# Chunk inverses of a recurrent mixer from blocks of sixteen rows, with shared products in its chunk steps

## The chip, the core and the metric

The kernel runs on one core of a Trainium2 chip. A core has five engines that work side by side, each through its own queue of instructions: TensorE (PE in the profile; its weight loads stand apart as PEld), VectorE (DVE), ScalarE (ACT), GpSimd (POOL) and SyncE (SP), which here issues the transfers. The time is the device time of one execution in microseconds.

## The reference, cut to what matters

The model is a long chain of layers over 512 tokens of width 1024. The change touches one of them, a mixer with 16 heads of width 64 whose state runs through the tokens:

```python
def step(state, inp):                      # state: heads x 64 x 64
    r_t, w_t, k_t, v_t, a_t, b_t = inp
    sa = jnp.einsum('bhij,bhj->bhi', state, a_t)
    state = (state * w_t[:, :, None, :] + sa[..., None] * b_t[:, :, None, :]
             + v_t[..., None] * k_t[:, :, None, :])
    y_t = jnp.einsum('bhij,bhj->bhi', state, r_t)
    return state, y_t
...
_, ys = lax.scan(step, state0, seq_inputs)  # one step per token
```

Then `ys` is normalised by head, gets a bonus term, is gated and goes through an output projection.

## The kernel before

The scan is done in chunks of 64 tokens. Within a chunk the corrections `sa` of its 64 tokens depend on each other through a triangular 64 x 64 matrix, and the kernel multiplies by that matrix's inverse. Two heads stand side by side on the 128 partitions (a head pair), so there are eight pairs `c` and eight chunks. Work comes in four units `u`: half `h = u // 2` of the tokens (four chunks `n`), and pairs 0 to 3 or 4 to 7. A unit has four parts:

- `rwkv_prep` and `rwkv_chunks`, for each pair: decays, keys and receptances (in `kr`), then products on TensorE into `G`, which holds for each chunk four 64 x 64 blocks: by `BK` (update vectors or keys) against `kr` (keys or receptances). L1583 are these products.
- `rwkv_inverse1`: the unit's 32 triangular blocks (4 pairs x 2 heads x 4 chunks) go through DRAM (`md`) so that a partition holds half of a matrix, 32 x 32. VectorE (GpSimd for unit 2) inverts these by 31 steps of two operations each (L1619, L1621). The results go back through DRAM into `G`, and a copy into `A11`.
- `rwkv_inverse2`: the off-diagonal 32 x 32 blocks, by two rounds of 32 small products (L1646, L1651), with a copy between them (L1648) and one after (L1653).
- `rwkv_steps`: four chunks in order, and in each the unit's four pairs. All its products go through the helper `mm` and show as L1665. For a pair and chunk they are, by the tiles on which they show: the residual, from the old state (`SB,kr`) and from `V` by two products (`ws`, 64*64), copied to `R` by L1688; the inverse applied (`R,ws`), copied by L1692; the new state, from the old one by a product with the identity (`SB,cst`, 128*128) and two products (`ws`, 128*64), scaled and copied by L1703; the output, from the old state (`SB,kr`) and two products (`ws`, 128*64), copied by L1710.

The instructions are written in the order of `rwkv` (L1465 to L1484), and a planner then orders each engine's queue by priorities and a simulated time; `steps` raises the priority of `rwkv_steps`. So preps, `rwkv_post` (normalising and gating of a finished unit) and the first products of the output projection lie in each queue among the steps. The steps start when the value projection `vproj` is done, since `UV` and unit 2's working set reuse the space of its inputs. A tag with n buffers (`bufs`) is handed out in turn: steps take two of three `mm` banks of the accumulators, the inverse's products the only `av` bank.

## Time and profile before

| | |
|---|---|
| median of 3 runs | 3906.36 us (3902.74 to 3907.86) |
| the profiled execution | 3908.79 us, span 3907.0 us |
| mean granted TensorE clock, of full speed | 0.956 |
| busy: PE, PEld | 3738.4 us (96%), 3000.4 us (77%) |
| busy: DVE, ACT, POOL | 1753.8 us (45%), 1507.1 us (39%), 1642.4 us (42%) |

Times in the rows count from the start of the span. An engine is busy while an instruction of it runs; matmuls are pipelined, so that one row's length is more than its distance to the next. An fp32 product shows as two records, and "x4" in a row is four records in a run. `64*128` means 64 rows of weights and 128 columns. The granted clock is 1.00 at 2.4 GHz and 0.50 at 1.2 GHz. A shown tile can be a larger buffer: `ws`, `wse` and `hn` are the units' working sets with `G`, `BK` and `UV`, `cst` the constants, `SB` the states, `av`, `mm`, `sc` and `tr` the accumulator banks.

### The profile page before, as it was taken

To read this page: it belongs to the slowest core of one execution; us is meant where nothing else is said; L and a number is where in the kernel's file an instruction comes from. 1 tells how busy PE (TensorE), PEld (TensorE's weight loads), DVE (VectorE), ACT (ScalarE), POOL (GpSimd) and SP (SyncE) were. 2 spreads that over 40 slices of the span, in tenths; PEclk is the share of its full clock that TensorE was granted. 3 is DMA by queue.
4 is the path that set the end of the run, shared out by engine and by line. 5 is a ranking of instruction groups with operands and counts; after the bars stand their busy time and mean duration, and the time that the engine had idled before them with its cause. 6 is when DMAs were issued, how large, how long until landed. Compare 5 with 4: busy or idle time off the path is not lost.

```text
span 3907.0 us, 48377 instructions
## 1 busy us (share of the span) xinstructions
PE 3738.4 (96%) x18540; PEld 3000.4 (77%) x18540; DVE 1753.8 (45%) x3587; ACT 1507.1 (39%) x2677; POOL 1642.4 (42%) x900
## 2 busy tenths in 40 slices
PE   9999999999999999999998899999899899799998
PEld 8766777888896677778886777888676777688887
DVE  4553254533545424544436655222568545534123
ACT  4433333433344333334334634332454433343322
POOL 4422436444453233444444563444534321543444
PEclk9999999999999999999998999999999557899999
DMA  5311214233342122232221332222222311321222
GB/s 190 116 54 49 89 60 135 87 97 97 120 152 81 55 67 71 87 114 97 97 95 62 99 106 76 86 93 95 99 85 88 73 41 42 124 102 63 96 97 87
DMA packets 148952, 354.10 MB, mean 91 GB/s; under 512 B 50080, under 2 KB 60864, under 8 KB 148464
## 3 DMA queue, kind: packets, MB, share of 16 engines
q1 hardware_dynamic: 148448, 350.18, 27.6%
q8 instruction: 146, 2.39, 0.3%
q0 software_dynamic: 272, 0.82, 0.1%
q14 instruction: 86, 0.70, 0.1%
HBM read 332.56 MB, written 18.38 MB: 90 GB/s over the span
## 4 chain that ended last, share of the span: by engine, by line
PE 76%; DVE 9%; DMA 5%; POOL 4%; ACT 3%; issue 3%; SPq 0%; POOLq 0%; DVEq 0%; ACTq 0%
PE mm L322 13%; PE mm L323 13%; PE mm L324 13%; PE mm L384 5%; PE mm L383 5%; PE mm L385 5%; PE mm L1665 4%; POOL wlo L285 2%; PE av L383 2%; PE av L385 2%; PE av L384 2%; PE sc L823 2%; PE av L652 1%; PE tr L843 1%; ACT whi L284 1%
## 5 line engine op out<-in xcount | busy, mean ns | idle before, releaser
L285 POOL TENSOR_TENSOR wlo<-wst,whi 128x1024 fp32r<-128x1024 f32 (+2 forms) x524 | 1260.2, 2408 | 1784.2 <-PE mm L324 900.9
L284 ACT ACTIVATE whi<-wst 128x1024 fp32r<-128x1024 f32 (+2 forms) x524 | 548.7, 1048 | 1100.0 <-DMA wst<-in_wu 153.1
L322 PE MATMUL mm<-xTh,whi 128*128 128x512 f32 (+1 forms) x2208 | 833.1, 379 | 13.1 <-ACT whi L284 10.1
L323 PE MATMUL mm<-xTl,whi 128*128 128x512 f32 (+1 forms) x2208 | 835.8, 379 | 0.6
L324 PE MATMUL mm<-xTh,wlo 128*128 128x512 f32 (+1 forms) x2208 | 833.2, 378 | 0.0
L322 PEld LDWEIGHTS mm<-xTh,whi 128*128 128x128 f32 x2208 | 416.6, 190 | 99.8 <-ACT whi L284 11.5
L324 PEld LDWEIGHTS mm<-xTh,wlo 128*128 128x128 f32 x2208 | 418.4, 190 | 84.0 <-issue 8.5
L323 PEld LDWEIGHTS mm<-xTl,whi 128*128 128x128 f32 x2208 | 418.5, 190 | 81.8 <-issue 6.8
L867 DVE SCALAR_TENSOR_TENSOR fup<-mm,vec,fup 128x510 f32<-128x510 f32 (+1 forms) x176 | 131.0, 747 | 220.1 <-ACT fup L865 217.1
L829 ACT ACTIVATE P<-sc,sm 128x128 f32<-128x128 f32 x192 | 100.7, 525 | 203.6 <-DVE sm L827 203.4
L826 DVE TENSOR_TENSOR sc<-sc,cst 128x128 f32<-128x128 f32 x192 | 56.3, 297 | 271.1 <-PE sc L825 256.4
L1160 DVE TENSOR_TENSOR relu<-relu,mm 128x512 f32<-128x512 f32 x64 | 43.8, 687 | 297.6 <-ACT relu L1159 297.6
L384 PE MATMUL mm<-wlo,ph 128*128 128x512 f32 x396 | 156.6, 395 | 0.0
L385 PE MATMUL mm<-whi,pl 128*128 128x512 f32 x396 | 154.6, 395 | 0.0
L383 PE MATMUL mm<-whi,ph 128*128 128x512 f32 x396 | 154.4, 396 | 0.0
L384 PE MATMUL mm<-wlo,xTh 128*128 128x512 f32 (+1 forms) x360 | 137.4, 382 | 5.2 <-POOL wlo L285 5.2
L385 PE MATMUL mm<-whi,xTl 128*128 128x512 f32 (+1 forms) x360 | 136.4, 380 | 0.0
L383 PE MATMUL mm<-whi,xTh 128*128 128x512 f32 (+1 forms) x360 | 132.8, 382 | 3.6 <-ACT whi L284 3.6
L1180 DVE TENSOR_TENSOR work<-work,mm 128x512 f32<-128x512 f32 x60 | 41.2, 687 | 168.1 <-PE mm L385 160.2
L968 PE MATMUL tr<-dg,work 128*128 128x128 f32 x384 | 61.9, 328 | 46.9 <-DVE rsq L416 16.0
L297 POOL TENSOR_TENSOR wres<-wst,wres 128x512 fp32r<-128x512 f32 (+1 forms) x56 | 83.7, 1512 | 37.1 <-ACT wres L296 32.2
L968 PEld LDWEIGHTS tr<-dg,work 128*128 128x128 f32 x384 | 58.8, 240 | 50.3 <-issue 33.6
(580 smaller groups left out, 7431.4 us busy)
## 6 DMA issues: line engine op xcount, KB each, us to landing
wst<-in_wu SPq DMA_DIRECT2D x88, 512.0 KB, 3.6
wst<-in_wmu SPq DMA_DIRECT2D x64, 512.0 KB, 3.6
wst<-in_wmd SPq DMA_DIRECT2D x64, 512.0 KB, 3.6
wst<-in_wg SPq DMA_DIRECT2D x48, 512.0 KB, 3.6
wst<-in_wn SPq DMA_DIRECT2D x44, 512.0 KB, 3.6
wst<-in_wa SPq DMA_DIRECT2D x24, 512.0 KB, 3.6
wst<-in_wb SPq DMA_DIRECT2D x24, 512.0 KB, 3.6
wst<-in_wd SPq DMA_DIRECT2D x24, 512.0 KB, 3.6
```

The source lines that it names most:

```text
L284: nc.scalar.activation(hi, st, AF.Copy)
L285: nc.gpsimd.tensor_sub(lo, st, hi.bitcast(F32))
L322: mm(out, lh, rh, start=start, stop=False)
L323: mm(out, lh, rl, start=False, stop=False)
L324: return mm(out, ll, rh, start=False, stop=stop)
L383: mm(o, xh, hi[:, s], start=k == 0, stop=False)
L384: mm(o, xh, lo[:, s], start=False, stop=False)
L385: mm(o, xl, hi[:, s], start=False, stop=k == nk - 1)
L829: nc.scalar.activation(P[:, o:o + n], sc[:, :n], AF.Exp, bias=mx[:, i:i + 1], accum_out=rs[:, i:i + 1])
L867: nc.vector.scalar_tensor_tensor(a[:, d:], ps[:, :512 - d], self.v(f"fc{l}{tap}", o + j), a[:, d:], op0=OP.mult, op1=OP.add)
L968: nc.tensor.matmul(ps[:, k * 128:k * 128 + 128], work[b][:, k * 128:k * 128 + 128], dg, start=True, stop=True)
L1665: ins = nc.tensor.matmul(*a, **kw, skip_group_check=True)
```

## The change

- The inverses start from blocks of 16 x 16 instead of 32 x 32: a partition of 128 holds a quarter of a matrix, and VectorE needs 15 steps of two operations. All four units' are on VectorE.
- The results go to DRAM (`dd`), and `rwkv_inverse2` fetches them and their transposes with 16 transfers into one pair of tiles, `D`, as the diagonal blocks of 32 x 32. Then 64 + 32 + 64 small products make the inverses of the 32 x 32 blocks before the two rounds that were there. `rwkv_inverse2` gets the raised priority too.
- In the steps one product of 128 columns makes the old state's part of residual and output together; `kr` and `G` are laid out for it. The output's other part uses the 64 rows of corrections alone, and VectorE adds the two.
- The new state's old part is a ScalarE copy with decay, made early; the product with the identity is gone, and VectorE adds the chunk's part to it in two operations.

```diff
@@ -108,7 +108,8 @@
     t = np.arange(64)[None, :]
-    c.add("g", np.concatenate([(s < t), (s <= t)], 1).astype(np.float32))
+    c.add("g", np.concatenate([(s <= t), (s < t), (s < t), (s <= t)], 1).astype(np.float32))
...
@@ -1334,10 +1336,13 @@
         nc.vector.tensor_scalar(om, self.vec[:, o:o + 48], -1.0, 1.0, op0=OP.mult, op1=OP.add)
         four = lambda name, dt=F32: self.g([128, 1024], "x4", 4, dt, name)
-        K["M"], K["A"] = four("M"), four("A")
+        ma, dd = four("MA"), four("D")
+        K["M"], K["A"] = ([ma[:, (2 * j + i) * 256:(2 * j + i + 1) * 256] for i in range(2)] for j in range(2))
+        K["D"] = [dd[:, i * 512:i * 512 + 512].rearrange("p (u s) -> p u s", u=16) for i in range(2)]
+        nc.gpsimd.memset(dd, 0.0)
         K["wa"], K["g"] = ([a[:, 0:512], a[:, 512:1024]] for a in (four("wa", F32R), four("hg", F32R)))
-        K["tmp"] = self.t([128, 256], "itmp", 1)
-        iv = K["iv"] = self.t([128, 256], "iv", 1)
+        K["tmp"] = self.t([128, 64], "itmp", 1)
+        iv = self.t([128, 256], "eb", 4, name="iv")
         b = [self.big([128, KC, S], F32R, f"mx{i}") for i in range(3)]
@@ -1345,8 +1350,9 @@
         q = lambda a, i, n: a[:, i * 512:(i + n) * 512]
         E = [self.t([128, 2048], "wse", 2) for _ in range(2)]
         K["SB"] = [[self.t([128, 128], "SB", 16) for _ in range(2)] for _ in range(8)]
-        for a, _ in K["SB"]:
-            nc.gpsimd.memset(a, 0.0)
+        for ab in K["SB"]:
+            for a in ab:
+                nc.gpsimd.memset(a, 0.0)
         def mix(j, k):
             m = self.t([128, 512], "ea", 4, name="mix")
...
@@ -1458,8 +1466,8 @@
             oT[h][q0:q0 + 4] = self.rwkv_post(q0, h, un(u))
         def steps(u):
-            self.rwkv_inverse2(u, un(u))
             with self.tc.high_priority(2000):
+                self.rwkv_inverse2(u, un(u))
                 self.rwkv_steps(u, un(u))
         inverse1(0)
@@ -1473,7 +1481,7 @@
         steps(0)
         prep(range(4), 1, True)
         steps(1)
-        inverse1(2, nc.gpsimd)
+        inverse1(2)
         post(0)
         prep(range(4, 8), 1, True)
         steps(2)
...
@@ -1516,6 +1524,18 @@
         nc.scalar.activation(hi, st, AF.Copy)
         nc.gpsimd.tensor_sub(lo, st, hi.bitcast(F32))
         return hi, lo
+
+    def kr_views(self, a):
+
+
+        return (a.rearrange("p (a w) -> p a w", a=2)[:, :, 64:192],
+                a.rearrange("p (a b s) -> p a b s", a=2, b=4)[:, :, 0::3, :])
+
+    def like(self, ap, i):
+
+        if i == 0:
+            return ap.rearrange("p (a w) -> p a w", a=2)
+        return ap.rearrange("p (a b s) -> p a b s", a=2, b=2)
     def rwkv_prep(self, c, h, after):
...
@@ -1554,19 +1575,20 @@
...
-        nc.vector.scalar_tensor_tensor(nk, r, self.v("rk", c), ta, op0=OP.mult, op1=OP.mult)
-        nc.gpsimd.tensor_mul(r, r, Pm)
+        for a in range(2):
+            nc.vector.scalar_tensor_tensor(lr(nk)[:, a], r[:, a], self.v("rk", c), lr(ta)[:, a], op0=OP.mult, op1=OP.mult)
+        nc.gpsimd.tensor_mul(r, r, lr(Pm))
@@ -1580,10 +1602,10 @@
             rr = slice(64 * g, 64 * g + 64)
             ps = self.bank("sc" if g else "tr")
             for n in range(4):
-                mm(ps[:, n * 128:n * 128 + 128], flat(BK[rr, n]), kr[rr, :, n * 64:n * 64 + 64],
+                mm(ps[:, n * 128:n * 128 + 128], flat(BK[rr, n]), kr[rr, n * 128:n * 128 + 128],
                    start=True, stop=True)
-            p3, mk = ps.rearrange("p (n s) -> p n s", n=4), K["gmask"].unsqueeze(1).to_broadcast([128, 4, 128])
-            nc.vector.tensor_mul(G[:, g], p3, mk)
+            p3, mk = ps.rearrange("p (n s) -> p n s", n=2), K["gmask"].unsqueeze(1).to_broadcast([128, 2, 256])
+            nc.vector.tensor_mul(G[:, g].rearrange("p (n m) s -> p n (m s)", m=2), p3, mk)
         tp = self.bank("tr")
         for t in range(2):
             mm(tp[:, 2 * t:2 * t + 2], s["rka"][:, t * 128:t * 128 + 128], self.hsel, start=True, stop=True)
@@ -1598,59 +1620,76 @@
         nc, K = self.nc, self.rk
         md = self.dr.tile([32, 64, 64], F32, name=f"md{u}")
-        ad = self.dr.tile([32, 32, 32], F32, name=f"ad{u}")
+        dd = self.dr.tile([2, 4, 32, 256], F32, name=f"dd{u}")
         eng = nc.sync
         G = K["ws"][u][1].rearrange("q (u x c) -> q u x c", u=16, x=2)
         us = [(64 * (1 - p), G[:, :, p], slice(16 * p, 16 * p + 16)) for p in range(2)]
         for u0, m, o in us:
-            eng.dma_start(md[o].rearrange("u s t -> s u t"), m[u0:u0 + 64, :, 0:64])
-        q0 = u % 2 * 64
-        q1 = slice(q0, q0 + 64)
-        M, A = (K[nm].rearrange("p (s t) -> p s t", s=32) for nm in "MA")
+            eng.dma_start(md[o].rearrange("u s t -> s u t"), m[u0:u0 + 64, :, u0:u0 + 64])
+        mf, af = K["M"][u % 2], K["A"][u % 2]
+        M, A = (a.rearrange("p (s t) -> p s t", s=16) for a in (mf, af))
         tmp = K["tmp"]
-        half, rows = (lambda b: slice(q0 + 32 * b, q0 + 32 * b + 32)), (lambda b: slice(32 * b, 32 * b + 32))
-        for b in range(2):
-            eng.dma_start(M[half(b)], md[:, rows(b), rows(b)])
-        nc.gpsimd.memset(K["A"][q1], 0.0)
-        nc.gpsimd.memset(K["A"][q1, 0::33], 1.0)
-        for s in range(31):
-            n, m = 31 - s, s + 1
-            t3 = tmp[q1, 0:n * m].rearrange("p (a b) -> p a b", a=n)
-            e.tensor_tensor(t3, M[q1, s, s + 1:].unsqueeze(2).to_broadcast([64, n, m]),
-                            A[q1, s, 0:m].unsqueeze(1).to_broadcast([64, n, m]), op=OP.mult)
-            ins = e.tensor_tensor(A[q1, s + 1:, 0:m], A[q1, s + 1:, 0:m], t3, op=OP.add)
-        eng.dma_start(ad, A[half(0)])
-        nc.scalar.activation(M[q1], A[q1].rearrange("p t s -> p s t"), AF.Copy)
-        for b in (1, 0):
-            eng.dma_start(md[:, rows(b), rows(b)], M[half(b)])
-        a = K["A11", u % 2] = self.t([128, 16, 32], "ksq", 2, name="A11")
-        for u0, m, o in us:
-            eng.dma_start(a[u0:u0 + 32], ad[o].rearrange("u s t -> s u t"))
-        for b in (1, 0):
-            for u0, m, o in us:
-                eng.dma_start(m[u0 + 32 * b:u0 + 32 * b + 32, :, 32 * b:32 * b + 32],
-                              md[o, rows(b), rows(b)].rearrange("u s t -> s u t"))
+        for b in range(4):
+            rows = slice(16 * b, 16 * b + 16)
+            eng.dma_start(M[32 * b:32 * b + 32], md[:, rows, rows])
+        nc.gpsimd.memset(af, 0.0)
+        nc.gpsimd.memset(af[:, 0::17], 1.0)
+        for s in range(15):
+            n, m = 15 - s, s + 1
+            t3 = tmp[:, 0:n * m].rearrange("p (a b) -> p a b", a=n)
+            e.tensor_tensor(t3, M[:, s, s + 1:].unsqueeze(2).to_broadcast([128, n, m]),
+                            A[:, s, 0:m].unsqueeze(1).to_broadcast([128, n, m]), op=OP.mult)
+            ins = e.tensor_tensor(A[:, s + 1:, 0:m], A[:, s + 1:, 0:m], t3, op=OP.add)
+        nc.scalar.activation(M, A.rearrange("p t s -> p s t"), AF.Copy)
+        for d, a in ((0, mf), (1, af)):
+            eng.dma_start(dd[d].rearrange("b u s -> (b u) s"), a)
+        K["dd", u] = dd
         return ins
     def rwkv_inverse2(self, u, sts):
         nc, K = self.nc, self.rk
         mm = nc.tensor.matmul
-        ps = self.bank("av")
-        Z = self.t([128, 512], "ea", 4, name="Z").rearrange("p (u s) -> p u s", u=16)
-        p4 = ps.rearrange("p (u s) -> p u s", u=16)
+        v3 = lambda ap: ap.rearrange("p (u s) -> p u s", u=16)
+        zt = lambda: v3(self.t([128, 512], "ea", 4, name="Z"))
         G = K["ws"][u][1].rearrange("q (u x c) -> q u x c", u=16, x=2)
         hf = [(slice(64 * (1 - p), 64 * (1 - p) + 32), slice(64 * (1 - p) + 32, 64 * (1 - p) + 64)) for p in range(2)]
+        quads = [(p, r) for p in range(2) for r in hf[p]]
+        X, XT = K["D"]
+        for d in (1, 0):
+            for b in range(4):
+                for p in range(2):
+                    r = 64 * (1 - p) + 16 * b
+                    nc.sync.dma_start(K["D"][d][r:r + 16, :, 16 * (b % 2):16 * (b % 2) + 16],
+                                      K["dd", u][d, b, 16 * p:16 * p + 16].rearrange("u (s t) -> s u t", s=16))
+        p1, Z1 = v3(self.bank("av")), zt()
+        for i in range(16):
+            for p, r in quads:
+                mm(p1[r, i], G[r, i, p, r], XT[r, i], start=True, stop=True)
+        nc.vector.tensor_tensor(Z1, p1, K["off"].unsqueeze(1).to_broadcast([128, 16, 32]), op=OP.mult)
+        p2, p3 = v3(self.bank("av")), v3(self.bank("sc"))
+        for i in range(16):
+            for p, (r, _) in enumerate(hf):
+                mm(p3[r, i], X[r, i], Z1[r, i], start=True, stop=True)
+        for i in range(16):
+            for p, r in quads:
+                mm(p2[r, i], Z1[r, i], X[r, i], start=True, stop=True)
+        a11 = self.t([128, 16, 32], "ksq", 2, name="A11")
+        for p, (r, _) in enumerate(hf):
+            nc.vector.tensor_add(a11[r], p3[r], XT[r])
+        for p, r in quads[::-1]:
+            nc.vector.tensor_add(G[r, :, p, r], p2[r], X[r])
+        p4, Z = v3(self.bank("av")), zt()
         for i in range(16):
             for p, (lo_, hi_) in enumerate(hf):
-                mm(p4[hi_, i], G[lo_, i, p, 32:64], K["A11", u % 2][lo_, i], start=True, stop=True)
+                mm(p4[hi_, i], G[lo_, i, p, hi_], a11[lo_, i], start=True, stop=True)
         for lo_, hi_ in hf:
             nc.scalar.activation(Z[hi_], p4[hi_], AF.Copy)
         for i in range(16):
             for p, (lo_, hi_) in enumerate(hf):
-                mm(p4[lo_, i], Z[hi_, i], G[hi_, i, p, 32:64], start=True, stop=True)
+                mm(p4[lo_, i], Z[hi_, i], G[hi_, i, p, hi_], start=True, stop=True)
         for p, (lo_, hi_) in enumerate(hf):
-            nc.vector.tensor_copy(G[lo_, :, p, 32:64], p4[lo_])
+            nc.vector.tensor_copy(G[lo_, :, p, hi_], p4[lo_])
     def rwkv_steps(self, u, sts):
@@ -1674,40 +1713,39 @@
             first, last = h == 0 and n == 0, h == 1 and n == 3
             UV = K["UV"][:, p, c0:c0 + 4]
             nc.sync.dma_start(UV[vr], V[ns].rearrange("s (c d) -> s c d", c=4))
-            S0 = [K["SB"][c0 + i][1 - p] for i in range(4)]
-
-            Yp, Rp = ([banks[i // 2][:, (2 * (i % 2) + j) * 128:(2 * (i % 2) + j) * 128 + 128] for i in range(4)]
-                      for j in range(2))
+            S0, S2 = ([K["SB"][c0 + i][a] for i in range(4)] for a in (1 - p, p))
+
+
+            A, B = ([banks[i // 2][:, (2 * (i % 2) + j) * 128:(2 * (i % 2) + j) * 128 + 128] for i in range(4)]
+                    for j in range(2))
             R = []
             for i, s in enumerate(sts):
                 if not first:
-                    mm(i, Rp[i][ur], s["kr"][:, 0, ns], S0[i], start=True, stop=False)
+                    mm(i, A[i], s["kr"][:, n * 128:n * 128 + 128], S0[i], start=True, stop=False)
                 for g, hs in enumerate(hs2):
-                    mm(i, Rp[i][ur, hs], s["G"][vr, g, n, 0:64], UV[vr, i, hs], start=first, stop=True)
-                R.append(self.t([128, 128], "R", 7))
-                nc.scalar.activation(R[i][ur], Rp[i][ur], AF.Copy)
+                    mm(i, A[i][:, hs], s["G"][vr, g, n, :], UV[vr, i, hs], start=first, stop=True)
+                R.append(self.t([128, 128], "R", 8))
+                nc.scalar.activation(R[i], A[i], AF.Copy)
+            if not first and not last:
+                for i, s in enumerate(sts):
+                    nc.scalar.activation(S2[i], S0[i], AF.Copy, scale=s["PC"][:, n:n + 1])
             for i, s in enumerate(sts):
                 for g, hs in enumerate(hs2):
-                    mm(i, Rp[i][ur, hs], s["G"][ur, g, n, 0:64], R[i][ur, hs], start=True, stop=True)
-                nc.scalar.activation(UV[ur, i], Rp[i][ur], AF.Copy)
+                    mm(i, B[i][ur, hs], s["G"][ur, g, n, ur], R[i][ur, hs], start=True, stop=True)
+                nc.scalar.activation(UV[ur, i], B[i][ur], AF.Copy)
             for i, s in enumerate(sts if not last else ()):
-                S2 = K["SB"][c0 + i][p]
-                if first:
-                    mm(i, Rp[i], s["BN"][:, n], UV[:, i], start=True, stop=True)
-                    for hs in hs2:
-                        nc.scalar.activation(S2[hs, hs], Rp[i][hs, hs], AF.Copy, scale=s["PC"][hs, n:n + 1])
-                    continue
-                mm(i, Rp[i], self.ident, S0[i], start=True, stop=False)
                 for hs in hs2:
-                    mm(i, Rp[i][hs, hs], s["BN"][:, n, hs], UV[:, i, hs], start=False, stop=True)
-                nc.scalar.activation(S2, Rp[i], AF.Copy, scale=s["PC"][:, n:n + 1])
+                    mm(i, B[i][hs, 0:64], s["BN"][:, n, hs], UV[:, i, hs], start=True, stop=True)
+                for hs in hs2:
+                    if first:
+                        nc.scalar.activation(S2[i][hs, hs], B[i][hs, 0:64], AF.Copy, scale=s["PC"][hs, n:n + 1])
+                    else:
+                        nc.vector.scalar_tensor_tensor(S2[i][hs, hs], B[i][hs, 0:64], s["PC"][hs, n:n + 1],
+                                                       S2[i][hs, hs], op0=OP.mult, op1=OP.add)
             for i, s in enumerate(sts):
-                if not first:
-                    mm(i, Yp[i][vr], s["kr"][:, 1, ns], S0[i], start=True, stop=False)
                 for g, hs in enumerate(hs2):
-                    mm(i, Yp[i][vr, hs], s["G"][:, g, n, 64:128], UV[:, i, hs], start=first, stop=True)
-                if p:
-                    nc.vector.tensor_copy(s["BN"][:, n // 2, :], Yp[i])
+                    mm(i, A[i][vr, hs], s["G"][ur, g, n, vr], UV[ur, i, hs], start=True, stop=True)
+                nc.vector.tensor_add(s["BN"][vr, n // 2, :], A[i][vr], R[i][vr])
         bk = K["ws"][u][0].rearrange("p (c n s) -> p c n s", c=4, n=4)
         for t in range(2):
             nc.sync.dma_start(bk[:, :, 2 + t], V[t * 128:t * 128 + 128].rearrange("s (c d) -> s c d", c=4))
```

## Rows read from the trace of the kernel before

**Rows 1.** The page: the clock granted to TensorE in 40 slices, tenths.
```profile
PEclk9999999999999999999998999999999557899999
```
**Rows 2.** Stretches: us; busy PE, PEld, DVE, ACT, POOL (instructions); clock; transfers' share, GB/s.
```profile
2957.00:3027.00 70.00, 62.30 (x307) 48.76 (x306) 67.29 (x140) 29.56 (x59) 37.05 (x22) 0.98 0.27 87
3027.00:3329.00 302.00, 280.08 (x2165) 222.34 (x2165) 152.24 (x410) 114.24 (x323) 80.43 (x133) 0.63 0.21 51
```
**Rows 3.** TensorE's waits, 3027 to 3329: total us, times, longest us.
```profile
PE av L1646 <- DMA A<-ad: 5.9, 3, 3.1
```
**Rows 4.** Sums by stretch: 3114 to 3233; then all six stretches at 2.4 GHz.
```profile
3114.10:3233.30 119.20, 117.41 (x728) 91.79 (x723) 53.30 (x150) 42.91 (x123) 29.50 (x53) 0.50 0.16 37
...
sum 74.00, PE 64.85 PEld 49.43 DVE 31.01 ACT 28.62 POOL 24.76; mean PE 10.81 PEld 8.24 DVE 5.17 ACT 4.77 POOL 4.13
```
**Rows 5.** TensorE's timeline at 1.2 GHz: start us, length us, line, what.
```profile
3200.09 2.08 PE L1583 MATMUL sc<-kr,wse 64*128 64x128 f32 x8
...
3205.43 0.63 PE L1665 MATMUL mm<-SB,kr 128*64 128x128 f32 x2
3205.99 0.69 PE L1665 MATMUL mm<-ws 64*64 64x64 f32 x4
3206.61 1.11 PE L1593 MATMUL tr<-cst,wse 128*128 128x128 f32 x4
...
3227.44 0.80 PE L1665 MATMUL mm<-SB,cst 128*128 128x128 f32 x2
3228.16 0.48 PE L1665 MATMUL mm<-ws 128*64 128x64 f32 x4
3228.58 0.80 PE L1665 MATMUL mm<-SB,cst 128*128 128x128 f32 x2
...
3230.00 0.63 PE L1665 MATMUL mm<-ws 128*64 128x64 f32 x4
3230.43 0.63 PE L1665 MATMUL mm<-SB,kr 128*64 128x128 f32 x2
3230.86 0.63 PE L1665 MATMUL mm<-ws 128*64 128x64 f32 x4
```
**Rows 6.** The same timeline just before 3260.7.
```profile
3259.64 0.44 PE L1665 MATMUL mm<-R,ws 64*64 64x64 f32 x4 [0.41 <-ACT R L1688]
...
3260.38 0.44 PE L1665 MATMUL mm<-ws 64*64 64x64 f32 x4
```
**Rows 7.** The same timeline: the inverse's products at 2.4 and 1.2 GHz.
```profile
3095.54 0.88 PE L1646 MATMUL av<-A,hn 32*32 32x32 f32 x42
...
3280.81 1.92 PE L1651 MATMUL av<-ws,Z 32*32 32x32 f32 x64
```
**Rows 8.** The same timeline: state products at 2.4 GHz.
```profile
3314.12 0.49 PE L1665 MATMUL mm<-SB,cst 128*128 128x128 f32 x2
3314.54 0.34 PE L1665 MATMUL mm<-ws,wse 128*64 128x64 f32 x4
3314.80 0.49 PE L1665 MATMUL mm<-SB,cst 128*128 128x128 f32 x2
```
**Rows 9.** The inverse's lines: ns min/median/max, first and last start us.
```profile
L1619 DVE TENSOR_TENSOR itmp<-M,A x93: 175/372/2424, 2962.9 to 3269.7; 64x31 f32<-64x31 f32 x6, 64x60 f32<-64x60 f32 x6, 64x87 f32<-64x87 f32 x6, 64x112 f32<-64x112 f32 x6
...
L1621 DVE TENSOR_TENSOR A<-A,itmp x93: 184/359/893, 2963.8 to 3270.7; 64x31 f32<-64x31 f32 x6, 64x60 f32<-64x60 f32 x6, 64x87 f32<-64x87 f32 x6, 64x112 f32<-64x112 f32 x6
```
**Rows 10.** The same of its copies and of a transfer's issue.
```profile
L1631 SPq DMA_DIRECT2D ws<-md x12: 432/487/584, 3034.8 to 3277.2; - x12
...
L1648 ACT ACTIVATE Z<-av x8: 588/589/590, 3040.4 to 3279.8; 32x512 f32<-32x512 f32 x8
...
L1653 DVE COPY ws<-av x6: 678/684/689, 3046.2 to 3283.5; 32x512 f32<-32x512 f32 x6
```
**Rows 11.** TensorE's timeline: unit 2's steps from their first inverse to their end.
```profile
3220.80 1.73 PE L1665 MATMUL mm<-R,ws 64*64 64x64 f32 x12
...
3267.78 0.79 PE L383 MATMUL mm<-whi,oT 128*128 128x512 f32 x1
```

More of the change, by code (lines that the diff above doesn't have):

```diff
@@ L110, in rwkv_consts @@
     t = np.arange(64)[None, :]
-    c.add("g", np.concatenate([(s < t), (s <= t)], 1).astype(np.float32))
+    c.add("g", np.concatenate([(s <= t), (s < t), (s < t), (s <= t)], 1).astype(np.float32))
+    c.add("off", ((np.arange(128)[:, None] % 32 >= 16) & (np.arange(32)[None, :] < 16)).astype(np.float32))
     c.add("sel", (np.arange(80)[None, :] == 14 + np.arange(128)[:, None] // 64).astype(np.float32))
@@ L1322, in rwkv @@
         nc = self.nc
-        cst = self.t([128, 464], "cst2", 1)
+        cst = self.t([128, 624], "cst2", 1)
         nc.gpsimd.dma_start(cst, self.I["cst2"])
         K = self.rk = {}
-        K["scan"], K["gmask"] = cst[:, 0:256], cst[:, 256:384]
-        sel = lambda m: cst[:, 398 - 2 * m:462 - 2 * m]
+        K["scan"], K["gmask"] = cst[:, 0:256], cst[:, 256:512]
+        K["off"] = cst[:, 512:544]
+        sel = lambda m: cst[:, 558 - 2 * m:622 - 2 * m]
         for nm, src, a, b in (("w0h", "w0", 0.5, 0.0), ("a0h", "a0", 0.5, 0.0), ("nkk", "kk", -1.0, 0.0),
@@ L1367, in raw @@
             return w
-        K["kr"] = [[self.rp.tile([128, 2, 256], F32, tag="rk", bufs=16, name="kr") for _ in range(8)]
+        K["kr"] = [[self.rp.tile([128, 512], F32, tag="rk", bufs=16, name="kr") for _ in range(8)]
                    for _ in range(2)]
@@ L1373, in evac @@
             for h in range(2):
-                nc.scalar.activation(K["kr"][h][m][:, i, :], ps[:, h * 256:h * 256 + 256], AF.Copy)
+                to = self.kr_views(K["kr"][h][m])[i]
+                src = ps[:, h * 256:h * 256 + 256]
+                nc.scalar.activation(to, self.like(src, i), AF.Copy)
         mk, mr, mv = [], [], []
@@ L1534, in rwkv_prep @@
         kr = K["kr"][h][c]
-        k, r = kr[:, 0, :], kr[:, 1, :]
+        k, r = self.kr_views(kr)
+        lk, lr = (lambda ap: self.like(ap, 0)), (lambda ap: self.like(ap, 1))
         r0, r1 = slice(0, 64), slice(64, 128)
@@ L1556, in rwkv_prep @@
             nc.sync.dma_start(nk[64 * g:64 * g + 64], K["ivd"][h, 2 * c + g:2 * c + g + 1].to_broadcast([64, 256]))
-        nc.vector.scalar_tensor_tensor(nk, k, cc("nkk"), nk, op0=OP.mult, op1=OP.mult)
+        nc.vector.scalar_tensor_tensor(lk(nk), k, cc("nkk"), lk(nk), op0=OP.mult, op1=OP.mult)
         bks = [BK[:, p::2, 1 - p, :] for p in range(2)]
@@ L1563, in rwkv_prep @@
         nc.vector.tensor_scalar(ta, ta, cc("ka1"), cc("ka2"), op0=OP.mult, op1=OP.add)
-        nc.vector.tensor_mul(ta, ta, k)
-        nc.vector.tensor_mul(k, nk, tw)
+        nc.vector.tensor_mul(lk(ta), lk(ta), k)
+        nc.vector.tensor_mul(k, lk(nk), lk(tw))
         for p in range(2):
             nc.vector.tensor_mul(BK[:, p::2, p, :], ch(ta)[:, p::2], ch(L)[:, p::2])
-        nc.vector.scalar_tensor_tensor(nk, r, self.v("rk", c), ta, op0=OP.mult, op1=OP.mult)
-        nc.gpsimd.tensor_mul(r, r, Pm)
+        for a in range(2):
+            nc.vector.scalar_tensor_tensor(lr(nk)[:, a], r[:, a], self.v("rk", c), lr(ta)[:, a], op0=OP.mult, op1=OP.mult)
+        nc.gpsimd.tensor_mul(r, r, lr(Pm))
         return dict(c=c, kr=kr, BK=BK, bk=bk, BN=BN, G=G, PC=PC, rka=nk,
```

## The prediction

> **What bounds the kernel now.** I read the page first: TensorE's granted clock dips to 5 and 7 tenths in slices 32 to 34 only [rows 1]. So the place to look is 3027 to 3329 us, the recurrent stage from the first chunk step to the last. Two sums by stretch follow [rows 2]. Before the stage, 2957 to 3027, TensorE is busy 62.3 of 70 us at a clock of 0.98 and VectorE 67.3 of 70: both nearly full. In the stage TensorE is busy 280.1 of 302 us at a mean clock of 0.63, VectorE only 152 us, ScalarE 114, GpSimd 80. TensorE's work sets the pace, with 21.9 us of idle time in all, of which the transfer ahead of the inverse's first products ends 5.9 [rows 3]. Whatever VectorE saves can reach the end only through that idle time and the 7.7 us before the stage.
>
> The third view is the clock by stretch. Six stretches, 74.0 us with 64.9 us of TensorE work, ran at 2.4 GHz; nearly all the rest, 3114 to 3233 for instance, ran at 1.2 GHz although TensorE was busy 117.4 of 119.2 us there [rows 4]. The timeline shows what went ahead: before the rise at 3233.4 stand state products (`SB,cst`) and output products (`SB,kr`, then `ws`), all on 128 rows [rows 5]; before the fall at 3260.7 stand mostly products on 64 rows (`R,ws` and `ws`, 64*64) [rows 6]. That order matters here, since the change takes away 128-row products.
>
> **The change part by part.** Prices are start to next start at 1.2 GHz; an fp32 product shows as two records.
>
> State and outputs [rows 5]. A state product with the identity takes 0.72 (3227.44 to 3228.16) and its two chunk products 0.42. An output's state product takes 0.43 (3230.00 to 3230.43 is the same length for its two chunk products). In a residual the state product takes 0.56 (3205.43 to 3205.99) and the two chunk products 0.62. There are 64 cases of head pair and chunk; 8 first ones have no old state, 8 last ones write none.
> - Output's own state product gone: 56 x 0.43 = -24.
> - Identity product gone: 48 x 0.72 = -35.
> - The shared state product is 128 columns wide instead of 64; I price it as the other 128*128 form, 0.72 for 0.56: 56 x 0.16 = +9.
> - Output chunk products go from 128 rows to 64, so to the 64*64 form, 0.62 for 0.43: 64 x 0.19 = +12.
> - First chunk's state: 8 x (0.42 - 0.72) = -2.
> - The shared residual product has 128 columns of weights and still 64 moving: unseen. Below, the same 0.62; above, L1583's form with 128 moving, 2.08 for eight, 1.0 for four: 0 to +24. The moving part is that of the 64*64 row, so I take +3.
> Together -37 us at 1.2 GHz, between -40 and -16.
>
> Small products. Each inverse now makes 32 + 32; it gets 64 + 32 + 64 more on blocks of 32, so 640 more, 1280 records. At 1.2 GHz 64 records took 1.92 us, 30 ns each; at 2.4 GHz 42 took 0.88, 21 ns [rows 7]. I take 30, as the stage is mostly at 1.2 GHz: +38 us, and not under 27. The Trainium skill, "TensorE: Matmul & The Clock Gate", Part 3, says that products at different 32-strips run at the same time; two of the new rounds use four positions where the old ones use two. By that, 1024 of the records would cost half, and the sum would be 15 us lower; no row here has four positions.
>
> So at an equal clock TensorE's work stays where it was: -37 + 38 = +1, between -13 and +22.
>
> The clock. The state pair at 2.4 GHz takes 0.42 + 0.26 = 0.68 against 1.14 [rows 5, 8], a factor of 1.68. The 64.9 us of work done at 2.4 GHz would cost 64.9 x 0.68 = 44 us more at 1.2. The change removes the identity products, one of two state products and the 128-row output products, which filled the time ahead of the rise; the 64- and 32-row products, which stand ahead of the falls, become most of the work. What stays on 128 rows is the pairs' state updates, post's transposes and the output projection. I let three quarters of the gain go: +33 us, between 0 and 44.
>
> VectorE. An inverse falls from 62 operations at medians of 372 and 359 ns [rows 9], 23 us, to 30, none of over 64 elements a partition: at the lower ends, 175 and 184 ns, some 5 us. Unit 2's, so far on GpSimd, comes over too, another 5. It gains two updates and one sum for each pair and chunk, for one copy in two; VectorE has 150 idle us in the stage, so I cost those at nothing; a step's update that stands behind post's operations in VectorE's queue delays that pair's next chunk, and TensorE has three other pairs meanwhile. ScalarE's decayed copy of the state lies ahead of the products that need it, and 188 idle us cover it. Ahead of the stage VectorE loses one chain, and TensorE may regain part of its 7.7 idle us: -3, from 0 to -6. The finer views of keys and receptances keep their element counts; the memsets, the wider mask and the split operation go to idle engines: nothing.
>
> Chains and queues. An inverse's own transfers before the products fall from 13 to 8, but 16 copies of blocks come behind, on SyncE's queue at 0.49 us each [rows 10]: 7.8 us in which the next V loads and weights wait. The products then make a chain: about 3.8, 0.7, 1.9, 3.8, four VectorE sums of 0.68, 1.9, two ScalarE copies of 0.59, 1.9 and two copies of 0.68 [rows 7, 10], some 19 us where the last four, 6.4 us, were. The single block buffer makes the next inverse's copies wait for these reads. Steps of other heads and preps lie beside it. The 5.9 us wait goes, smaller ones come: -5, between -15 and +15.
>
> Sum: 1 + 33 - 5 - 3 = +26 us. The profiled execution took 3908.8 (span 3907.0 and 1.8 around it), 2.4 over the median. 3908.8 + 26 - 2.4 = 3932.
>
> **The rivals.**
> - *The clock keeps its stretches* (0.22). Post's transposes and projection work could lie among the steps often enough. Then 1 - 5 - 3 = -7 us, 3899; with small products at 21 ns another 11 less, 3888. It ends faster from the point where, at that low price, less than 10 of the 44 us is lost. Against it: 119 us of nearly gapless work at 1.2 GHz, with more 128-row work than will be left.
> - *The clock is high throughout* (0.04). If TensorE only had to be without gaps, the freed VectorE would let it stay at 2.4 GHz: the 215.2 us of work at 1.2 would take 128, about 3820. The Trainium skill, same page, "Why this matters for your kernels", has that rule: keep the engine continuously busy, avoid gaps. The trace disagrees: 117.4 of 119.2 us busy, and no rise [rows 4].
> - *The last inverse becomes the bound* (0.12). Now unit 3's inverse (VectorE to 3270.7, last copy at 3283.5) lies mostly under unit 2's steps (3220.8 to 3267.8) [rows 9 to 11]. The inverse products now have the steps' high priority; if unit 2 runs ahead of unit 3's preps, its 5 + 7.8 + 19, with transfers some 40 us, lie bare, less about 15 of post and projection (my estimate): +25 more, 3957.
> - *It cancels* (0.10). VectorE was never on the path and products only change places: 3906, either side.
> - My forecast has the rest, 0.52, with its own range of 3912 to 3960.
>
> **How the numbers follow.** Within 0.2% (7.8 us) a measurement can't tell this kernel from no change. Slower: 0.46 of the forecast and 0.12 of the bare inverse, 0.58. Faster: 0.13 of the kept clock, 0.04 and 0.05 of the cancelling, 0.22. Same: the remaining 0.06, 0.09 and 0.05, 0.20. The range leaves out the high clock and the far ends: 3892 (the kept clock, with part of the low price) to 3960 (weight loads at their upper bound, or a bare inverse).
>
> **What would show it.** Granted clock over the stage near 0.55 instead of 0.63; identity products gone; 128*128 `SB,kr` records near 0.36 us apart; 1792 records on 32 x 32 with spacing of 20 to 30 ns; VectorE's work in the stage under 130 us; TensorE busy about 310 us until the last step. The prediction is wrong if the clock stays at 0.63 or above, if small products cost under 20 ns at 1.2 GHz, or if the steps' end comes before 3320.

## The result, and the profile after

The changed kernel takes 3935.5 us (median of 4 runs) against 3905.3 for the kernel before: ratio 1.0077 (95% interval 1.006 to 1.0095), some 30 us slower. The profiled execution took 3932.95, the forecast was 3932. The number held; its terms held only in part.

The page's clock row, as in [rows 1], now dips to 5 and 6 tenths in three slices in a row:

```profile
PEclk9999999999999999999998999999898556899999
```

Sums by stretch, columns as in [rows 2]. Of the changed kernel: from the fall of the clock to the end of the last step product, then the sum of the four stretches at 2.4 GHz inside that. Then, from the first step product to the last (the measure used for the experiments), the changed kernel and the kernel before:

```profile
3025.80:3357.20 331.40, 311.42 (x3122) 254.57 (x3122) 167.43 (x522) 105.02 (x312) 45.58 (x69) 0.57 0.15 38
...
sum 44.70, PE 40.18 PEld 31.25 DVE 27.14 ACT 23.07 POOL 18.01; mean PE 10.04 PEld 7.81 DVE 6.78 ACT 5.77 POOL 4.50
...
3019.50:3357.20 337.70, 314.64 (x3269) 257.40 (x3268) 169.81 (x534) 108.34 (x320) 47.54 (x70) 0.58 0.16 40
...
3030.60:3329.30 298.70, 280.25 (x2168) 222.55 (x2168) 151.30 (x405) 111.76 (x321) 80.73 (x133) 0.63 0.21 50
```

The stage grew from 302.0 to 331.4 us: the last step product ends at 3357.2 instead of 3329.3, 28 us later. About 4 us of that come back behind the stage, as the profiled executions differ by 24.2. Idle time did not do it (331.4 - 311.4 = 20.0 us, before 21.9). TensorE is busy 31.3 us longer, in part because the clock is lower, 0.57 for 0.63. Of the work done at 2.4 GHz 40.2 us are left of 64.9 [rows 4].

TensorE's waits from 3025.8 to 3353.4, total us, times, longest. The copy wait of [rows 3] is gone, VectorE's state addition is the new first one:

```profile
PE mm L1704 <- DVE SB L1743: 7.0, 8, 2.0
PE av L1685 <- DVE ws L1681: 5.5, 2, 3.9
PE av L1690 <- ACT Z L1687: 2.4, 1, 2.4
PE mm L1704 <- DMA ws<-vd: 2.2, 1, 2.2
```

TensorE's timeline at 1.2 GHz (start us, length us), answering to [rows 5] and [rows 7]: three small-product runs of an inverse, then a shared state product, the shared residual product and the next pair's state product:

```profile
3028.02 1.85 PE L1673 MATMUL sc<-Z,D 32*32 32x32 f32 x61
...
3029.72 1.92 PE L1676 MATMUL av<-D,Z 32*32 32x32 f32 x126
3037.15 1.92 PE L1685 MATMUL av<-A,ws 32*32 32x32 f32 x64 [3.93 <-DVE ws L1681]
...
3182.56 0.79 PE L1704 MATMUL mm<-SB,kr 128*128 128x128 f32 x2
3183.29 1.11 PE L1704 MATMUL mm<-ws,hn 64*128 64x64 f32 x4
3184.33 0.79 PE L1704 MATMUL mm<-SB,kr 128*128 128x128 f32 x2
```

The shared state product takes 0.73 us (3182.56 to 3183.29), as priced. The four records of the residual's chunk product take 1.04, where the kernel before took 0.62 with 64 columns of weights [rows 5]: just over the upper bound (1.0), where the prediction stayed near the lower. The two-position rounds stay at 30 ns a record (1.92 / 64, 1.85 / 61), the four-position round is at 15 (1.92 / 126).

The weight loads from 3025.8 to 3353.4, by form (busy us, mean ns over both clocks), say why the residual's product is dear:

```profile
L1704 PEld LDWEIGHTS mm<-ws 64*128 64x128 f32 x180 | 40.1, 308 | 9.5 <-issue 9.0
...
L1704 PEld LDWEIGHTS mm<-ws 64*64 64x64 f32 x184 | 21.7, 202 | 9.5 <-DVE SB L1743 4.3 <-DVE ws L1748 1.2 <-DVE wse L1748 1.0
...
L1704 PEld LDWEIGHTS mm<-ws,wse 128*64 128x64 f32 x176 | 12.1, 191 | 9.3 <-DVE SB L1743 4.0 <-ACT ws L1735 1.3 <-issue 0.6
```

The first two are followed by the same 64 moving columns. The Trainium skill, "TensorE: Matmul & The Clock Gate", section "LDWEIGHTS (loading the stationary operand)", has the load's time go with the columns of the weights and not with their rows. The trace agrees: 308 against 202 ns on the same 64 rows, and 191 ns on 128 rows with 64 columns.

### The profile page after: what moved, and what is told of

Same layout as the page of the kernel before. It is cut to its first block, busy times and chain, and to the rows that moved or that the text cites. A ratio compares the mean times of both kernels' runs of the same rounds, so it can differ in the third digit from the quotient of the medians.

```text
span 3931.2 us, 50693 instructions
## 1 busy us (share of the span) xinstructions
PE 3765.1 (96%) x19628; PEld 3032.3 (77%) x19628; DVE 1730.6 (44%) x3693; ACT 1502.8 (38%) x2677; POOL 1603.7 (41%) x847
## 3 DMA queue, kind: packets, MB, share of 16 engines
q1 hardware_dynamic: 145952, 348.61, 26.1%
## 4 chain that ended last, share of the span: by engine, by line
PE 79%; DVE 8%; DMA 4%; POOL 4%; issue 3%; ACT 3%; SPq 0%; POOLq 0%; DVEq 0%; ACTq 0%
PE mm L323 13%; PE mm L325 13%; PE mm L324 13%; PE mm L385 5%; PE mm L384 5%; PE mm L386 5%; PE mm L1704 4%; POOL wlo L286 3%; PE av L384 2%; PE av L386 2%; PE av L385 2%; PE sc L824 2%; PE av L653 1%; PE tr L844 1%; ACT whi L285 1%
```

## The experiments

All were timed in five rounds against the kernel before on the same chip; ratios are to those runs. In us the difference is the ratio's times 3907. The fence of each is TensorE's stretch from its first step product to its last, columns as in [rows 2]. Three causes stood against each other: the clock (my forecast's), the small products' own time, and the wide weights' own time.

The last three columns are of TensorE in the steps of the one profiled execution: its clock, its busy time at 2.4 GHz, and its work counted as at 1.2 GHz, which is all its busy time plus 0.68 times that at 2.4 GHz (the prediction's factor of 1.68; the changed kernel and 8, with the same products, come out at 344 and 346). The whole clock is the mean clock of an execution from start to end, median of all executions.

| kernel | ratio (95%) | against before, us | whole clock | clock in the steps | busy at 2.4 GHz, us | work as at 1.2 GHz, us |
|---|---|---|---|---|---|---|
| kernel before | 1 | 0 | 0.954 to 0.957, by chip | 0.63 | 66.0 | 325 |
| changed kernel | 1.0077 (1.006 to 1.0095) | +30 | 0.946 | 0.58 | 43.4 | 344 |
| 1 inverses only | 1.0004 (0.999 to 1.0019) | +2 | 0.960 | 0.68 | 98.1 | 352 |
| 2 state by VectorE only | 0.9974 (0.9962 to 0.9986) | -10 | 0.956 | 0.62 | 53.4 | 296 |
| 3 all but the inverses | 1.0056 (1.0038 to 1.0073) | +22 | 0.9455 | 0.53 | 19.3 | 314 |
| 4 narrow residual | 1.0034 (1.0023 to 1.0046) | +13 | 0.9465 | 0.54 | 26.1 | 321 |
| 5 split state product | 1.0064 (1.0052 to 1.0076) | +25 | 0.946 | 0.55 | 30.8 | 338 |
| 6 inverses and VectorE's state | 0.9965 (0.9952 to 0.9977) | -14 | 0.957 | 0.64 | 72.9 | 331 |
| 7 useless products added | 1.0155 (1.0141 to 1.0168) | +61 | 0.941 | 0.54 | 28.6 | 380 |
| 8 inverse's products late | 1.0097 (1.0084 to 1.011) | +38 | 0.944 | 0.54 | 22.4 | 346 |
| 9 nothing shared, new layout | 1.003 (1.0018 to 1.0043) | +12 | 0.951 | 0.61 | 65.2 | 337 |
| 10 as 9, wide weights | 1.0122 (1.0104 to 1.0139) | +48 | 0.943 | 0.54 | 24.2 | 357 |
| 11 as 2, inverse first | 0.9979 (0.9966 to 0.9991) | -8 | 0.955 | 0.59 | 41.0 | 297 |
| 12 as 6, state products side by side | 1.0026 (1.0012 to 1.0039) | +10 | 0.9485 | 0.56 | 35.1 | 313 |

One kernel's clock differs from execution to execution, and its time with it: on one chip the kernel before took from 3892.8 us at a whole clock of 0.961 to 3920.0 at 0.952. A step of 0.002 in the whole clock is one of some 0.03 in the steps (0.002 x 3907 / 300), so differences of that size in the column of the steps show nothing by themselves.

**1. Inverses only.** The kernel before takes the new `rwkv_inverse1` and `rwkv_inverse2` on its own mask layout:

```diff
-            self.rwkv_inverse2(u, un(u))
             with self.tc.high_priority(2000):
+                self.rwkv_inverse2(u, un(u))
...
-        inverse1(2, nc.gpsimd)
+        inverse1(2)
```

> The kernel before with the new inverses alone (blocks of sixteen rows, all four on VectorE, their products at high priority); the steps keep the identity product, the own state product of the outputs and their 128-row chunk products. Small products theory (the added products are the loss, by their own time): the two kernels' traces give 42.6 us of small products against 16.4, so +26 us, 3931 us, with the stage's clock unchanged near 0.63. Clock theory (mine: TensorE's work stays level, the 128-row products that go take the 2.4 GHz stretches with them): the 128-row products stay, so most of the stretches stay, clock above 0.60, and the added products cost their own +18 to +28, 3923 to 3933. Weights theory (the residual product with 128 columns of weights is the loss, +24 us): the small products are paid back by VectorE's relief, no more than +8, under 3914.

```profile
3012.90:3317.80 304.90, 284.99 (x3452) 228.97 (x3451) 134.08 (x398) 105.50 (x319) 46.04 (x69) 0.68 0.17 41
```

No difference, though 1280 records came in (3452 for 2168): the clock over the steps rose to 0.68. (The profiled execution, 3901.2, lies 7 us under its median.) Counted as at 1.2 GHz the work grew by 26 us, and the higher clock paid for it. That the small products alone are the loss falls with this; 32-row products came in and the clock did not fall.

**2. State by VectorE only.** From the kernel before:

```diff
-                mm(i, Rp[i], self.ident, S0[i], start=True, stop=False)
...
-                    mm(i, Rp[i][hs, hs], s["BN"][:, n, hs], UV[:, i, hs], start=False, stop=True)
-                nc.scalar.activation(S2, Rp[i], AF.Copy, scale=s["PC"][:, n:n + 1])
+                    mm(i, Rp[i][hs, 0:64], s["BN"][:, n, hs], UV[:, i, hs], start=True, stop=True)
+                for hs in hs2:
+                    nc.vector.scalar_tensor_tensor(S2[hs, hs], Rp[i][hs, 0:64], s["PC"][hs, n:n + 1],
+                                                   S2[hs, hs], op0=OP.mult, op1=OP.add)
```

> The kernel before with one part of the change: the decayed old state is copied by ScalarE and added by VectorE, so 48 identity products (96 records of 352 ns at 1.2 GHz, 204 at 2.4; 29 us as they ran) go, the rest stays. If the clock did not depend on these products: -25 to -29 us, 3876 to 3880, stage's clock 0.62 or more. Clock theory: the stretches at 2.4 GHz shrink from 74 us, the stage's clock falls under 0.60 and half or more of the gain is lost, 3887 to 3900.

```profile
3029.90:3321.90 292.00, 259.62 (x2072) 206.78 (x2073) 178.04 (x502) 112.45 (x321) 81.04 (x133) 0.62 0.21 51
```

Faster by 10 us. Of the 29 us of products that go, 280.3 - 259.6 = 20.7 show as less busy time; the clock falls by 0.01 only, where the clock theory wanted under 0.60; idle time grows from 18.4 to 32.4 us. More than half of the gain was lost, more of it to waits (14 us) than to the clock (12.6 us of work left 2.4 GHz, which is worth some 9).

**3. All but the inverses.** The changed kernel with the inverses, their priority and the GpSimd chain of the kernel before.

> The changed kernel with the inverses of the kernel before (its priority for them and its GpSimd chain too); the shared products and VectorE's state stay. Small products theory: all 26 us of extra small products go and nothing else was lost, 3909 us or less. Weights theory: the steps' products at 1.2 GHz are 202 us of records against 217, the loss must come from elsewhere if they were all; with the clock of before kept it would be -16 to -10, 3890 to 3895. Clock theory: the gain of 16 is met by up to 33 us lost at 2.4 GHz, so it stays at 3905 to 3922, with the stage's clock under 0.58.

```profile
3031.90:3352.00 320.10, 300.48 (x1975) 243.54 (x1975) 182.18 (x541) 112.24 (x321) 82.14 (x133) 0.53 0.19 47
```

22 us slower: more than any theory had, the clock theory nearest with 17 and a clock under 0.58. Against experiment 2 it has the sharing with its layout in addition, and that is +32 us. In the profiled steps 18 us of it are more work (314 for 296), and 34 us of work left 2.4 GHz, which is worth 23; idle time fell by 13. So work and clock both lose here.

**4. Narrow residual.** From the changed kernel (in this one the outputs lose the old state's share, so it is read for its time alone):

```diff
-                    mm(i, A[i][:, hs], s["G"][vr, g, n, :], UV[vr, i, hs], start=first, stop=True)
+                    mm(i, A[i][ur, hs], s["G"][vr, g, n, ur], UV[vr, i, hs], start=first, stop=True)
...
-                    mm(i, A[i][vr, hs], s["G"][ur, g, n, vr], UV[ur, i, hs], start=True, stop=True)
+                    mm(i, A[i][vr, hs], s["G"][:, g, n, vr], UV[:, i, hs], start=first, stop=True)
```

> The changed kernel, but the residual's chunk product has 64 columns of weights again and the output's chunk product is on 128 rows again, as before; the shared state product, VectorE's state and the new inverses stay. Weights theory: 256 records go from 250 to 144 ns and 256 from 144 to 107 at 1.2 GHz, 27 + 9 = -36 us, 3899, at an unchanged clock of 0.56. Clock theory: the same, and the 256 records on 128 rows bring some of the 2.4 GHz stretches back: 3880 to 3899 with the stage's clock at 0.58 or more. Small products theory: nothing to gain in the steps, 3930 to 3936.

```profile
3022.40:3348.10 325.70, 303.16 (x3269) 241.85 (x3268) 168.69 (x534) 109.73 (x321) 48.63 (x70) 0.54 0.17 41
```

(1.0077 - 1.0034) x 3907 = 17 us come back of the 36 expected; the work falls by 23. The clock did not go up with 256 records on 128 rows put back: 0.54 for 0.58 in the profiled execution (the slowest of twelve), and a whole clock level with the changed kernel's. Both theories had this wrong.

**5. Split state product.** From the changed kernel:

```diff
-                    mm(i, A[i], s["kr"][:, n * 128:n * 128 + 128], S0[i], start=True, stop=False)
+                    for x in (ur, vr):
+                        mm(i, A[i][x], s["kr"][:, n * 128 + x.start:n * 128 + x.stop], S0[i], start=True, stop=False)
```

> The changed kernel with the shared state product (128 columns of weights, 128 moving) taken apart again into two of 64 columns of weights and 128 moving each; everything else stays. At a fixed clock that only adds work: 112 records of 362 ns become 224 of about 255, +16 us, 3951 us. Clock theory: these products are what brings 2.4 GHz; more than the 16 us comes back, 3915 to 3935, with the steps' time at 2.4 GHz at 70 us or more against 51 in the changed kernel.

```profile
3019.50:3361.70 342.20, 317.48 (x3381) 252.63 (x3380) 172.02 (x535) 109.03 (x320) 47.96 (x70) 0.55 0.16 40
```

Not to be told from the changed kernel, at the same whole clock. The added work was not there either: in the timeline at 1.2 GHz two such products take 0.62 us together, where one standing alone took 0.43 to 0.56 [rows 5] and the 128-column one 0.73:

```profile
3195.39 0.69 PE L1704 MATMUL mm<-SB,kr 128*64 128x128 f32 x4
3196.01 1.11 PE L1704 MATMUL mm<-ws,hn 64*128 64x64 f32 x4
```

**6. Inverses and VectorE's state.** The edits of 1 and 2 together.

> The kernel before with two parts of the change: the new inverses and VectorE's addition of the old state; residuals and outputs keep products of their own. By the two parts alone (0 and -10 us) 3898 us. Clock theory: 3890 to 3902, with 70 us or more at 2.4 GHz in the steps. If the parts hinder each other (the inverse's products at high priority once VectorE is also on the steps' path), 3905 or more.

```profile
3019.00:3323.50 304.50, 281.78 (x3365) 227.00 (x3364) 161.45 (x494) 108.63 (x320) 46.84 (x69) 0.64 0.18 43
```

Faster than both kernels, 14 us under the one before. What is left of the change, the sharing with its layout, then costs 14 + 30 = 44 us beside these two.

**7. Useless products added.** To the changed kernel, behind each residual:

```diff
+                if not first:
+                    mm(i, B[i][vr], s["kr"][:, n * 128 + vr.start:n * 128 + vr.stop], S0[i], start=True, stop=True)
```

> The changed kernel with 56 useless products (128 rows, 64 columns of weights, 128 moving: the output's own state product of before, its result never read) after each residual. At a fixed clock: 112 records of about 255 ns at 1.2 GHz, +28 us, 3963 us. Clock theory: the time at 2.4 GHz in the steps grows from 51 to 70 us or more and gives half or more of that back, 3937 to 3950.

```profile
3018.10:3399.00 380.90, 360.80 (x3381) 286.80 (x3380) 170.69 (x534) 109.05 (x320) 48.74 (x70) 0.54 0.14 35
```

By the ratios 30 us over the changed kernel: the products' whole price at 1.2 GHz and nothing back. More work on 128 rows did not bring the clock here.

**8. Inverse's products late.** From the changed kernel:

```diff
+            self.rwkv_inverse2(u, un(u))
             with self.tc.high_priority(2000):
-                self.rwkv_inverse2(u, un(u))
...
-        inverse1(2)
+        inverse1(2, nc.gpsimd)
```

> The changed kernel with the inverse's products and block copies out of the steps' high priority, and unit 2's chain on GpSimd, as they stood before. If the order of the inverses costs time: 3925 us or less and the steps' last product 8 us or more earlier. Clock theory: the order is not the loss, 3931 to 3940.

```profile
3020.30:3374.40 354.10, 330.62 (x3260) 270.55 (x3259) 167.09 (x504) 107.43 (x319) 54.69 (x99) 0.54 0.15 35
```

By its ratio 8 us slower than the changed kernel, and the intervals overlap: the new order was no loss. The steps' clock reads 0.54 for 0.58 with the same products, but the whole clocks, 0.944 and 0.946, lie within the scatter of one kernel: that order alone moves the clock is not shown.

**9 and 10. Nothing shared on the new layout, and wide weights alone.** From the changed kernel for 10; for 9 the chunk product's weights are `s["G"][vr, g, n, ur]` and its result `A[i][ur, hs]`:

```diff
-                    mm(i, A[i], s["kr"][:, n * 128:n * 128 + 128], S0[i], start=True, stop=False)
+                    mm(i, A[i][ur], s["kr"][:, n * 128 + ur.start:n * 128 + ur.stop], S0[i], start=True, stop=False)
...
+                if not first:
+                    mm(i, A[i][vr], s["kr"][:, n * 128 + vr.start:n * 128 + vr.stop], S0[i], start=True, stop=False)
                 for g, hs in enumerate(hs2):
-                    mm(i, A[i][vr, hs], s["G"][ur, g, n, vr], UV[ur, i, hs], start=True, stop=True)
-                nc.vector.tensor_add(s["BN"][vr, n // 2, :], A[i][vr], R[i][vr])
+                    mm(i, A[i][vr, hs], s["G"][:, g, n, vr], UV[:, i, hs], start=first, stop=True)
+                nc.vector.tensor_copy(s["BN"][vr, n // 2, :], A[i][vr])
```

> The changed kernel with nothing shared: outputs have their own state product (64 columns of weights) and chunk products on 128 rows, residuals 64 columns of weights; the new inverses, VectorE's state and the new layout of keys, receptances and masks stay. If the sharing is the whole loss: as the kernel with the new inverses and VectorE's state on the old layout, ratio 0.9965, some 3895 to 3903, with 70 us or more at 2.4 GHz in the steps. If the layout costs something by itself: above 3908.

```profile
3020.90:3339.60 318.70, 293.07 (x3381) 234.03 (x3380) 167.68 (x534) 109.63 (x321) 48.87 (x70) 0.61 0.17 42
```

> The same, but the residual's chunk products take all 128 columns of weights; the half of their result that the outputs would have shared is never read. Not a column more is moved through TensorE. Weights theory: 256 records go from some 148 to 250 ns at 1.2 GHz, +17 to +26 us at the clock of its pair. Clock theory, joined to it: slower work of this kind also takes stretches at 2.4 GHz away (to 40 us or less of them), so +30 us or more against its pair. If the records' 250 ns came from what stands around them and not from the weights: within 8 us of its pair.

```profile
3026.10:3383.60 357.50, 340.90 (x3372) 278.04 (x3371) 169.52 (x534) 109.63 (x319) 46.20 (x69) 0.54 0.14 35
```

The pair differs in the columns of the weights alone: (1.0122 - 1.003) x 3907 = 36 us. In the profiled steps the work grows by 20 us (357 for 337), 41 us of work left 2.4 GHz, which is worth 28, and idle time falls by 9. Number 9 also stands 25 us over number 6, so the new layout costs something by itself: views of keys and receptances, masks, and one result for residual and output, which VectorE empties each chunk. Which of these was not tried apart.

**11. As 2, with the inverse's products at high priority.** The first hunk of experiment 1 on experiment 2.

> The kernel before with VectorE's state alone (ratio 0.9974) and the inverse's products at the steps' high priority, as the changed kernel has them. In the changed kernel this order was worth 17 us; if it works here too, 3885 to 3892. If the order only acted through which products stand beside which, and so through the clock, anything from 3890 to 3905.

```profile
3026.40:3327.50 301.10, 269.18 (x2072) 214.38 (x2072) 178.67 (x501) 112.83 (x321) 81.10 (x133) 0.59 0.21 50
```

No difference to experiment 2. The 17 us in its expectation compared medians of two chips; by ratios it was 8.

**12. As 6, the output's state product beside the residual's.**

```diff
+                    mm(i, Rp[i][vr], s["kr"][:, 1, ns], S0[i], start=True, stop=True)
...
-                if not first:
-                    mm(i, Yp[i][vr], s["kr"][:, 1, ns], S0[i], start=True, stop=False)
...
+                    nc.vector.tensor_add(s["BN"][vr, n // 2, :], Yp[i][vr], R[i][vr])
```

> The kernel with the new inverses and VectorE's state on the old layout (ratio 0.9965), with the output's own state product moved to stand right behind the residual's, both of 64 columns of weights and on different halves of the result; ScalarE's copy takes both halves and VectorE adds the state's share to the output at the end. In the kernel with the shared product taken apart such a pair cost 2 x 156 ns for each of its two rounds at 1.2 GHz; where the two stood apart, 2 x 260. At the pair's price 224 records of 156 instead of 260 ns at 1.2 GHz (153 to 90 at 2.4): -19 us, and of that half or more stays if the clock moves: 3878 to 3892, ratio 0.9915 to 0.995. If the nearness of the two products was not the reason for the price: 3900 or more.

```profile
3013.60:3333.70 320.10, 289.42 (x3356) 225.16 (x3355) 168.13 (x526) 107.63 (x319) 45.35 (x69) 0.56 0.16 39
```

The price came as expected; the timeline shows the pair at 0.63 us:

```profile
3202.30 0.70 PE L1688 MATMUL mm<-SB,kr 128*64 128x128 f32 x4
3202.93 0.69 PE L1688 MATMUL mm<-ws,hn 64*64 64x64 f32 x4
```

Yet it is (1.0026 - 0.9965) x 3907 = 24 us slower than 6. The work fell by 18 us, from 331 to 313; the clock fell from 0.64 to 0.56 (the whole clock from 0.957 to 0.9485), with 38 us of work less at 2.4 GHz, and idle time rose from 22.7 to 30.7 us. Work saved on TensorE came out as lost time.

## Why the prediction was right in sum, and where its terms were not

The place and the end of it held: TensorE's pace in the stage, busy 311 us (said about 310), clock 0.57 (said 0.55), the loss visible at the last step. By its terms:

- *State, outputs, first chunk* held: identity and own state products gone, the shared one at 0.73 us.
- *The shared residual product*, "I take +3", is the step that failed. I priced it by its moving part; its weights set it (10 against 9). By the rows it is 64 x (1.04 - 0.62) = +27 us, a little over the bound of 24. The 64*128 row of L1583 was the nearer one.
- *Small products*, +38, were too dear. From start to next start at 1.2 GHz over the whole stage the four-position rounds took 21 ns on average, just above the 20 that the prediction had named as a sign against it, and the other new one 31: 1024 x 0.021 + 256 x 0.031 = +29 us. The Trainium skill, "TensorE: Matmul & The Clock Gate", Part 3, which the prediction weighed and did not take, has products at different positions run at the same time. The trace agrees: 15 ns with four positions in an unbroken run, 30 with two.
- So at an equal clock the parts make -37 - 3 + 27 + 29 = +16 in place of +1. The stage's sums say nearly the same: all work at 1.2 GHz would be 280.1 + 0.68 x 64.9 = 324 us before and 311.4 + 0.68 x 40.2 = 339 after, +15.
- *The clock*, +33, was too much: 64.9 - 40.2 = 24.7 us of work left 2.4 GHz, times 0.68 is +17.
- *Idle*, -5, and *before the stage*, -3, came out at -2 and about -1. Sum at the last step: 15 + 17 - 2 - 1 = +29, where 28 were measured. *Behind the stage*, at which the prediction put nothing, 4 came back, to 24. Work 14 us too cheap and a clock 16 us too dear cancelled: that the number came so near is luck.
- *The rivals* did not come: no wait puts the last inverse on the path, and the clock neither kept its stretches nor stayed high.
- VectorE's work in the stage was to be under 130 us; it is 167.4. The state updates and output sums, which I counted and never summed, are 27.1 + 13.2 + 4.5 = 45 us of it (groups by form: busy us, mean ns, idle before):

```profile
L1743 DVE SCALAR_TENSOR_TENSOR SB<-mm,PC,SB 64x64 f32<-64x64 f32 x96 | 27.1, 283 | 41.9 <-PE mm L1704 40.5
L1748 DVE TENSOR_TENSOR wse<-mm,R 64x128 f32<-64x128 f32 x46 | 13.2, 287 | 38.8 <-PE mm L1704 38.4
...
L1748 DVE TENSOR_TENSOR ws<-mm,R 64x128 f32<-64x128 f32 x16 | 4.5, 288 | 14.8 <-PE mm L1704 14.6
```

These wait for TensorE far longer than TensorE for the state additions (7.0 us).

The reason given for the clock, that products on 128 rows bring it and those on 64 and 32 rows take it, is not shown and as a rule is wrong: experiment 1 added 32-row products and the clock rose, 4 and 7 put 128-row products back and it did not rise. It rested on few rows: between those of [rows 5] and the rise at 3233.4 the kernel before has products on 64 rows too.

```profile
3231.84 0.69 PE L1665 MATMUL mm<-ws 64*64 64x64 f32 x4
```

Shown is that the loss is about half work (+15) and half clock (+17). The wide weights bring both (10 against 9). That the clock can take more than the work gives is shown by 12 against 6: 18 us less work, and 24 us later, of which 8 are idle time. What in the stream of products decides the clock stays open: the kernels at 0.59 or more in the steps, 0.951 or more over the whole, all use 64 columns of weights for residuals and state products apart; every kernel that joins one of the two, or sets the state products side by side, is at 0.58 and 0.9485 or less.

Neither the inverses nor VectorE's addition made it slower: together they gain 14 us (beside the sharing, 3 against the changed kernel, the inverses cost at most some 8, with intervals that overlap). The sharing with its layout loses 44, and the ratios take it apart: the layout alone +25 (9 against 6), the wide weights +36 (10 against 9), and -18 for the joined state product with the outputs' shorter products (the changed kernel against 10). Beside narrow residuals the joined product gained nothing (4 against 9, +13 and +12).

## What to carry to other kernels

Price a small product by its weights as well as by what it moves: doubling the weights' columns to save a product can cost more than the product. Where the granted clock moves inside a stage, a part that saves work is not a gain until it is timed with the parts around it, and parts are to be timed one by one: here two gained 14 us together and the third, with the layout it needed, lost three times that.

## What the runs showed of the hardware

- Two products of 64 columns of weights with the same 128 moving columns, written to different halves of the result, take 0.62 us together at 1.2 GHz when they stand side by side, less than the single product of 128 columns (0.73).
- From 3060 to 3328 us of experiment 10 TensorE was busy 261.95 of 268.00 us, and its clock stayed at 0.50: a nearly full engine did not get 2.4 GHz (row below). The rule in the Trainium skill, "TensorE: Matmul & The Clock Gate", "Why this matters for your kernels", to keep the engine busy without gaps, was not enough for these products.
- Executions of one kernel differ in the clock that they are granted, and in time with it: on one chip the kernel before took 3892.8 us at a mean clock of 0.961 and 3920.0 at 0.952.

```profile
3060.00:3328.00 268.00, 261.95 (x2394) 213.22 (x2393) 128.33 (x401) 83.02 (x245) 28.62 (x46) 0.50 0.12 27
```
